# Row-by-row output projection of a cross-attention block, in a fixed order, in front of a SwiGLU layer

## The chip, the cores and the metric

The kernel runs on one core of one Trainium2 chip. The metric is the device time of one execution in microseconds (us). A core has five engines that run their own instruction streams: TensorE for matrix products and transpositions (PE in the profile, with PEld for its weight loads), VectorE (DVE), ScalarE (ACT), GpSimd (POOL) and SyncE (SP), which here only issues DMA transfers. Matrix products are written into PSUM, which the kernel uses as eight banks of 128 partitions x 512 numbers of 32 bits.

## The reference, cut to what matters

The reference is one encoder layer of width 1024 over 512 tokens: two mixers merged by gates, a cross-attention to 256 memory tokens, and a SwiGLU. The change touches the stretch from the softmax of the cross-attention to the first products of the SwiGLU:

```python
def memory_cross_attention(hn, memn, w_q, w_k, w_v, w_o):
    ...
    s = jnp.einsum('blhd,bmhd->bhlm', q, k).astype(jnp.float32) * (XATTN_HEAD_DIM ** -0.5)
    p = jax.nn.softmax(s, axis=-1).astype(v.dtype)
    o = jnp.einsum('bhlm,bmhd->blhd', p, v).reshape(bsz, seq, D_MODEL)
    return o @ w_o

def swiglu(hn, w_gate, w_up, w_down):
    return (jax.nn.silu(hn @ w_gate) * (hn @ w_up)) @ w_down
...
        h = h + memory_cross_attention(rms_norm(h, xattn_norm_g[i]), memn,
                                       w_q[i], w_k[i], w_v[i], w_xo[i])
        h = h + swiglu(rms_norm(h, ffn_norm_g[i]), w_gate[i], w_up[i], w_down[i])
```

Four heads of 256 are used; the SwiGLU is 2816 wide. `w_o` is called `w_xo` in the kernel.

## The kernel before, in words

**Number format.** Every operand of a product is split into a high part in a rounded 32-bit format and the rest. `split` (L80) does it: a cast on ScalarE (L85), then a subtraction on VectorE (L86) that needs the cast's result. `mm3` (L375) makes three matmuls of one product: high x high, high x low, low x high.

**Seven products in place of eight.** The large products are done in blocks of a 2 x 2 scheme with seven products instead of eight. In `w_xo`'s case each of the seven has a number q, which the comments and this text call P1 to P7. The sum of products that makes one quarter of the output is collected in PSUM, and `onto` (L1416) adds a pair of PSUM banks to two row blocks of the residual `h` (or subtracts them), on VectorE (L1421). Token rows come in four blocks of 128, t = 0 to 3; columns in two halves of 512. The sum in the banks `ox` that is subtracted from rows 2 and 3, second half, by `onto(ox, 2, 1, ALU.subtract)` is called U here.

**Order of the projection.** After heads 2 and 3 the products of `w_xo` run in this order, each in two parts c = 0 and 1 with a weight block of 256 x 512 each: P6 in `ox`, P5 in `oq`, P4 in `oy`, P2 in `ov`, P3 in `oq`. `oq` is begun by P5, added to rows 0 and 1, and then P3 is added on top of it in the same banks and the whole goes to rows 2 and 3. The PSUM pools have five banks for products (tag "mm": `ox`, `oq`, `ov`, later `pf`, `px`, `pv` and so on) and three auxiliary ones (tag "aux": `oy1` and the transpositions `ptr`). A new pair of banks has to wait until the tile that held the bank before has been read: `ov` takes the banks of `ox`.

**Norm and transposition.** As soon as a row block of `h` is complete, `half_done` squares and sums each half on ScalarE (`sum_sq`, L500). `to_fn(t, ...)` makes the norm factor on VectorE and GpSimd (L509 to L511), the scaled row `xs` on VectorE (two instructions, L526), and then, a little later by the kernel's own count of TensorE's time (`later`, `tick`), the transpositions: eight blocks of 128 x 128 in two auxiliary banks `ptr` (L534), each split into `fn` (L85, L86) and also copied whole to `full` by ScalarE (L538). A bank of `ptr` is free again when cast, subtraction and copy have read it.

**After it.** The SwiGLU begins with the rows 0 and 1 (`T0`): `gate_part(0, T0)` and `gate_part(1, T0)` (tile `pf`), and between them the first unit of the seven-product scheme (`px`, then `pv`). Then `between` (a matmul into a bank `idle`, L1567), the same gate blocks for rows 2 and 3, and a block of the up projection. The next products are `pq`.

**Who sets the order.** The kernel is written with a tile scheduler. The program text gives dependencies and priorities; a planner with costs of its own orders the instructions of each engine. Instructions passed through `in_order` keep, on their engine, the order of the program text among themselves. While `pinned[0]` is true, that holds for both halves of every `split`, for every square of `sum_sq`, and for the additions of `onto`; matmuls are pinned only where `mm3` is called with `turn`. `pinned[0]` becomes true before P6's last additions and false before the additions of P2's `ov` to rows 2 and 3.

**Weights.** `next_w` hands out the next weight block of one list, `plan`. It issues the loads that lie up to 15 blocks ahead, as far as each load's own lead allows (3 blocks for `w_xo`), and splits the blocks that lie up to 2 ahead. So a call of `next_w` also issues transfers on SyncE's queue and the two halves of a split on ScalarE and VectorE. Weight blocks of P4 to P7 are sums that were put in DRAM earlier (`xsum`); those of P2 and P3 come straight from `w_xo`. The tile names are `wraw` for the raw block, `whi` and `wlo` for its halves, `b11`, `b21`, `t`, `b22` for those of the SwiGLU units, and `s` for a block of w_gate that is kept split.

**Softmax.** `scores(hd)` multiplies each of the four rows of a head's exponentials by the reciprocal of their sum: on VectorE for heads 0 and 1 (L1274), on ScalarE for heads 2 and 3 (L1276).

Of the kernel before, what the change touches and what calls it, by code (L numbers as in the profile page):

```python
# [12 lines left out]
ALU = mybir.AluOpType  # L13
# [39 lines left out]
def hybrid_layer_kernel(  # L53
# [8 lines left out]
    nc = tc.nc  # L62
    x, mem, out = x[0], mem[0], out[0]
    w_in, w_glu, w_proj_a, w_proj_b, w_out = w_in[0], s5_w_glu[0], w_proj_a[0], w_proj_b[0], w_out[0]
    w_q, w_k, w_v, w_xo = w_q[0], w_k[0], w_v[0], w_xo[0]
# [11 lines left out]
    def bank(name):  # L77
        return pm.tile([P, 512], F32, tag="mm", name=name)
# [13 lines left out]
    pinned = [False]  # L92
    in_order = tc.keep_in_program_order
# [253 lines left out]
    def next_w(*key):  # L347
        i = used_w[0]
        used_w[0] += 1
        assert len(plan[i][0]) == len(key) and plan[i][0][1:] == key[1:] and plan[i][0][0] is key[0]  # L350
        for j in range(i, min(i + FAR + 1, len(plan))):
            begin(j, i)
            if j - 1 >= len(tiles) and j - 1 <= i + SPLITS:
                split_w(j - 1)
        for j in range(len(tiles), min(i + SPLITS + 1, len(plan))):
            split_w(j)
        tile_, tiles[i] = tiles[i], None
        return tile_

    def begin(j, i):  # L360

        loads = plan[j][1]
        while loads and j - loads[0][0] <= i:
            loads.pop(0)[1]()
# [4 lines left out]
    def split_w(j):  # L369
        tiles.append(plan[j][2]())  # L370

    def mm3(ps, a, b, start, stop, free=False, turn=False):

        for i, (x, y) in enumerate(((0, 0), (0, 1), (1, 0))):
            m = nc.tensor.matmul(ps, a[x], b[y], start=start and i == 0, stop=stop and i == 2, skip_group_check=free)  # L375
            if turn:
                in_order(m)
# [26 lines left out]
    def feat_block(ps, x, act, nk, kpt, tsl, fresh=True):  # L404

        kb, hi, lo = x
        for j in range(2):
            cs = slice(j * P, (j + 1) * P)
            for k in range(kpt):
                kk = kb + k  # L410
                mm3(ps[j][:, tsl], (hi[:, k, cs], lo[:, k, cs]), (act[0][:, kk, tsl], act[1][:, kk, tsl]),
                    kk == 0 and fresh, kk == nk - 1, not fresh)
# [57 lines left out]
    def tick(us=5.2):  # L470

        side["now"] += us / 5.2
        run_due()
        side["credit"] = min(side["credit"] + us * side["rate"], us)
        while side["credit"] > 0.0 and side["gen"] is not None:
            try:
                used = next(side["gen"])
            except StopIteration:
                side["gen"] = None
                return  # L480
            if used is None:
                side["credit"] = 0.0
                return
            side["credit"] -= used
# [13 lines left out]
    def sum_sq(dst, src):  # L498
        sq = np_.tile([P, 512], F32, tag="ev", name="sq", bufs=2)
        act = nc.scalar.activation(sq[:, :src.shape[-1]], src, AF.Square, accum_out=dst)  # L500
        if pinned[0]:
            in_order(act)
# [11 lines left out]
    HALF = (slice(0, 512), slice(512, 1024))  # L514
# [32 lines left out]
    def slot(tag, shape, dt, name):  # L547
        return sp.tile(list(shape), dt, tag=tag, name=name)
# [511 lines left out]
    for h in range(H):  # L1060
        ps = bank("psv")
# [84 lines left out]
    h = slot("A", (P, NT, D), F32, "h")  # L1146
# [27 lines left out]
    hss = cp.tile([P, 3, NT, 2], F32, name="hss")  # L1174
# [12 lines left out]
    def feat_norm(g, hi, lo, full=None, skip=False):  # L1187

        return lambda t, ss: norm_feat(h[:, t, :], g, hi, lo, slice(t * P, (t + 1) * P), ss, full,
                                       0 if skip and t >= 2 else None)  # L1190
# [60 lines left out]
    def scores(hd):  # L1251
        q_hi, q_lo = qs.pop(hd)
        scale = XD ** -0.5
        prob = ap_.tile([P, NT, M], F32, tag="prob", name="prob", bufs=1) if hd % 2 == 0 else \
            np_.tile([P, NT, M], F32, tag="gain", name="prob", bufs=2)
        for i in range(2):
            ps = bank("psc").rearrange("p (t m) -> p t m", t=2)
            for tt in range(2):
                t = 2 * i + tt
                tsl = slice(t * P, (t + 1) * P)  # L1260
                for k in range(2):
                    mm3(ps[:, tt, :], (q_hi[:, k, tsl], q_lo[:, k, tsl]),
                        (kt_hi[:, 2 * hd + k, :], kt_lo[:, 2 * hd + k, :]), k == 0, k == 1)
            mx, nm, sm, rs = (ap_.tile([P, 2], F32, tag=k, name=k, bufs=4) for k in ("mx", "nm", "sm", "rs"))
            nc.vector.tensor_reduce(mx, ps, AX.X, ALU.max)
            nc.vector.tensor_scalar(nm, mx, -scale, None, ALU.mult)
            for tt in range(2):
                nc.scalar.activation(prob[:, 2 * i + tt, :], ps[:, tt, :], AF.Exp, bias=nm[:, tt:tt + 1],
                                     scale=scale, accum_out=sm[:, tt:tt + 1])
            nc.vector.reciprocal(rs, sm)  # L1270
            for tt in range(2):
                row = prob[:, 2 * i + tt, :]
                if hd < 2:
                    nc.vector.tensor_scalar(row, row, rs[:, tt:tt + 1], None, ALU.mult)  # L1274
                else:
                    nc.scalar.activation(row, row, AF.Copy, scale=rs[:, tt:tt + 1])  # L1276
        return prob
# [20 lines left out]
    def product(ps, u, q, start, ops):  # L1298

        hi, lo = next_w(u[0], u[1], q)  # L1300
        for j in range(2):
            cs = slice(j * P, (j + 1) * P)
            for k in range(4):
                a = (hi[:, k, cs], lo[:, k, cs])
                b = (ops[q][0][:, k, :], ops[q][1][:, k, :])
                for i, (x, y) in enumerate(((0, 0), (0, 1), (1, 0))):
                    nc.tensor.matmul(ps[:, j, :], a[x], b[y], start=start and j == k == i == 0,  # L1307
                                     stop=k == 3 and i == 2, skip_group_check=True)
        tick(2.7)
# [95 lines left out]

    g_f = gain(ffn_norm_g[0], "g_f")

    def xo_product(ps, q, c, start, stop, w=None, ts=(0, 1)):
        hi, lo = w or next_w(w_xo, q, c)
        a = xops[q]  # L1410
        for t in ts:
            tsl = slice(t * P, (t + 1) * P)
            for k in range(2):
                mm3(ps[t], (a[0][:, 2 * c + k, tsl], a[1][:, 2 * c + k, tsl]), (hi[:, k, :], lo[:, k, :]),
                    start and k == 0, stop and k == 1, True)
        tick(1.35 * len(ts))  # L1416

    def onto(ps, t0, half, op):
        for t in range(2):
            hs = h[:, t0 + t, HALF[half]]  # L1420
            add = nc.vector.tensor_tensor(hs, hs, ps[t], op)  # L1421
            if pinned[0]:
                in_order(add)

    def half_done(t, half):
        sum_sq(hss[:, 1, t, half:half + 1], h[:, t, HALF[half]])
# [7 lines left out]
    ox = [bank("ox0"), bank("ox1")]  # L1434
# [19 lines left out]
    oq = [bank("oq0"), bank("oq1")]  # L1454
# [8 lines left out]
    for t in range(2):  # L1463
        half_done(t, 1)
    onto(ox, 0, 0, ALU.add)
    xo_product(oy, 4, 0, False, False)
    onto(ox, 2, 1, ALU.subtract)
    xo_product(oy, 4, 1, False, True)
    onto(oy, 0, 0, ALU.add)
    for t in range(2):  # L1470
# [5 lines left out]
    to_fn = feat_norm(g_f, fn_hi, fn_lo, full)  # L1476
    for t in range(2):
        to_fn(t, hss[:, 1, t, :])
    xo_product(ov, 2, 1, False, True)
    pinned[0] = False  # L1480
    onto(ov, 2, 0, ALU.add)
    for t in (2, 3):
        half_done(t, 0)
    ws = [next_w(w_xo, 3, c) for c in range(2)]
    for c in range(2):
        xo_product(oq, 3, c, False, c == 1, ws[c])
    onto(oq, 2, 1, ALU.add)
    for t in (2, 3):
        half_done(t, 1)
        to_fn(t, hss[:, 1, t, :])  # L1490

# [49 lines left out]
    def put(u, f, ts, src):  # L1543
        dst = acts(u[1] // 512, f)[:, :, ts]
        if u[0] is w_gate:
            nc.scalar.activation(dst, src, AF.Silu)
        else:
            nc.vector.tensor_tensor(dst, dst, src, ALU.mult)

    def unit_second(u, v):  # L1550
        product(v, u, 2, False, ops)
        put(u, 0, T0, v)
# [3 lines left out]
    ps = [bank("pf0"), bank("pf1")]  # L1556
    ws = []

    def gate_part(i, ts):
        if ts is T0:  # L1560
            ws.append((4 * i,) + next_w(w_gate, 4 * i, 4, FS, 256))
        feat_block(ps, ws[i], fn, KD, 4, ts, ts is T0)
        tick(2.7)

    def between():

        in_order(nc.tensor.matmul(aux("idle"), ops[1][0][:, 0, 0:P], fn_hi[:, 4, :], start=True, stop=True))  # L1567

    gate_part(0, T0)
    begun = unit_start(UNITS[0])  # L1570
    gate_part(1, T0)
    unit_second(UNITS[0], begun[1])
    between()
    for i in range(2):
# [53 lines left out]
    for i, u in enumerate(UNITS):  # L1628
        final = i == len(UNITS) - 1
        x, v = begun  # L1630
        q = unit_bank("pq")
# [164 lines left out]
```

## Time and profile before

| | us |
| --- | --- |
| median of 3 runs | 912.39 (910.86 to 913.31) |
| profiled execution | 911.88 |
| its span | 910.1 |
| PE busy | 890.3 (98%) |
| DVE busy | 641.6 (70%) |
| ACT busy | 491.0 (54%) |
| POOL busy | 111.9 (12%) |

The mean granted clock of TensorE over the span was 0.995 of full speed. Times inside the profile are microseconds from the start of the span. A row of the timeline has the start, the length, the engine, the line of the kernel, the operation, `output<-inputs`, the tile's shape, how many instructions the row holds, and in brackets the idle time before it and what ended that. A row of the waits has the waiting engine, tile and line, what it waited for, and then the total, the number and the longest. A row of the windows has the window, its length, then busy time and number of instructions for PE, PEld, DVE, ACT and POOL, TensorE's granted clock, the share of the DMA engines and GB/s.

The change lies between about 500 us (softmax of heads 2 and 3) and 612 us (first products of the SwiGLU). In the stretch from 540 to 612 the matmuls of `w_xo`, the transpositions and the first SwiGLU products follow each other on PE with five waits.

### The profile page before, as it was taken

The numbers are of one execution on the slowest core, as the hardware profiler recorded it, in microseconds if no ns is written. First come the engines' busy times: TensorE is split into PE (matmuls) and PEld (weight loads), VectorE is DVE, ScalarE is ACT, GpSimd is POOL, SyncE is SP. The second block draws the span as 40 slices with busy tenths as digits, with TensorE's granted clock in tenths as the row PEclk, the third lists the DMA queues.
The fourth block names the chain that finished last, engine by engine and source line by source line (L and its number), as shares of the span: only waits on it lengthen the run. The fifth ranks groups of instructions, "written<-read, shape, count | busy, mean of one in ns | idle before, by whom it ended". The sixth has DMA issues, their size and how long they took to land.

```text
span 910.1 us, 14545 instructions
## 1 busy us (share of the span) xinstructions
PE 890.3 (98%) x5619; PEld 784.7 (86%) x5619; DVE 641.6 (70%) x1040; ACT 491.0 (54%) x724; POOL 111.9 (12%) x173
## 2 busy tenths in 40 slices
PE   9999999999999999999999998899999999999996
PEld 6888888888888887889899987799999999986885
DVE  5696652888753235858956798866778777897875
ACT  5543985144364334347655785635455455654663
POOL 1004320110025200011001000101121011000010
PEclk9999999999999999999999999999999999999999
DMA  7567574586546578873568446718799998366673
GB/s 243 165 162 179 122 185 141 162 194 154 153 136 143 134 197 242 274 212 120 180 216 257 133 139 175 217 34 223 177 276 214 214 234 229 93 197 190 205 242 104
DMA packets 116167, 165.35 MB, mean 182 GB/s; under 512 B 13873, under 2 KB 78913, under 8 KB 116034
## 3 DMA queue, kind: packets, MB, share of 16 engines
q1 hardware_dynamic: 95234, 134.56, 46.0%
q0 software_dynamic: 18272, 28.81, 19.0%
q10 hardware_dynamic: 2592, 1.05, 0.4%
q8 instruction: 44, 0.72, 0.3%
q14 instruction: 25, 0.20, 0.1%
HBM read 157.61 MB, written 46.63 MB: 224 GB/s over the span
## 4 chain that ended last, share of the span: by engine, by line
PE 85%; ACT 5%; DVE 4%; DMA 3%; issue 2%; POOL 1%; ACTq 0%; POOLq 0%; SPq 0%; DVEq 0%
PE pf L375 27%; PE px L1307 12%; PE pt L375 11%; PE pq L1307 6%; PE dx L375 5%; PE pv L1307 3%; PE qx L1307 2%; PE dq L375 2%; PE pk L815 2%; DMA wraw<-dsum 1%; ACT whi L85 1%; DVE wlo L86 1%; PE ptr L534 1%; PE po L375 1%; PE ox L375 1%
## 5 line engine op out<-in xcount | busy, mean ns | idle before, releaser
L86 DVE TENSOR_TENSOR wlo<-wraw,whi 128x1024 fp32r<-128x1024 f32 (+1 forms) x147 | 174.7, 1188 | 106.1 <-ACT whi L85 104.3
L85 ACT CAST whi<-wraw 128x1024 fp32r<-128x1024 f32 (+1 forms) x147 | 150.4, 1025 | 166.7 <-PE pf L375 70.5
L375 PE MATMUL pf<-xn,whi 128*128 128x512 f32 x448 | 140.1, 392 | 0.0
L375 PEld LDWEIGHTS pf<-xn,whi 128*128 128x128 f32 x448 | 83.4, 188 | 17.1 <-issue 0.2
L375 PE MATMUL pf<-xn,wlo 128*128 128x512 f32 x224 | 87.4, 390 | 0.0
L1307 PE MATMUL px<-fn,whi 128*128 128x256 f32 x480 | 83.2, 276 | 0.0
L1307 PEld LDWEIGHTS px<-fn,whi 128*128 128x128 f32 x480 | 72.7, 188 | 0.2
L85 ACT CAST whi<-b 128x1024 fp32r<-128x1024 f32 x40 | 42.1, 1054 | 49.3 <-PE px L1307 27.8
L86 DVE TENSOR_TENSOR wlo<-b,whi 128x1024 fp32r<-128x1024 f32 x40 | 48.8, 1221 | 26.0 <-ACT whi L85 26.0
L1307 PE MATMUL px<-fn,wlo 128*128 128x256 f32 x240 | 66.3, 276 | 0.0
L1307 PE MATMUL pq<-s,whi 128*128 128x256 f32 x320 | 55.0, 276 | 0.0
L375 PE MATMUL dx<-whi,s 128*128 128x512 f32 x170 | 53.6, 391 | 0.4 <-ACT whi L85 0.4
L85 ACT CAST whi<-t 128x1024 fp32r<-128x1024 f32 x30 | 31.6, 1053 | 34.1 <-PE pv L1307 10.6
L86 DVE TENSOR_TENSOR wlo<-t,whi 128x1024 fp32r<-128x1024 f32 x30 | 36.7, 1224 | 18.7 <-ACT whi L85 18.7
L375 PEld LDWEIGHTS pf<-xn,wlo 128*128 128x128 f32 x224 | 42.1, 188 | 8.7
L1307 PEld LDWEIGHTS pq<-s,whi 128*128 128x128 f32 x320 | 48.3, 188 | 0.0
L1307 PEld LDWEIGHTS px<-fn,wlo 128*128 128x128 f32 x240 | 45.1, 188 | 0.0
L1307 PE MATMUL pq<-s,wlo 128*128 128x256 f32 x160 | 44.2, 276 | 0.0
L375 PE MATMUL pt<-whi,xn 128*128 128x512 f32 x128 | 43.6, 412 | 0.1
L375 PEld LDWEIGHTS dx<-whi,s 128*128 128x128 f32 x170 | 31.8, 188 | 7.4 <-ACT whi L85 0.8
L375 PE MATMUL dx<-wlo,s 128*128 128x512 f32 x85 | 32.9, 390 | 0.0
L295 POOL DMA_DIRECT2D dsum<-in_w_down_dram x12 | 13.9, 1158 | 134.9 <-DMA dsum<-in_w_down_dram 130.1
(456 smaller groups left out, 2266.4 us busy)
## 6 DMA issues: line engine op xcount, KB each, us to landing
wraw<-in_w_in_dram SPq DMA_DIRECT2D x36, 512.0 KB, 4.6
dsum<-in_w_down_dram SPq DMA_DIRECT2D x20, 512.0 KB, 5.3
wraw<-dsum SPq DMA_DIRECT2D x20, 512.0 KB, 4.1
b<-in_w_gate_dram SPq DMA_DIRECT2D x15, 512.0 KB, 4.7
b<-in_w_up_dram SPq DMA_DIRECT2D x15, 512.0 KB, 4.9
wraw<-in_w_down_dram SPq DMA_DIRECT2D x15, 512.0 KB, 4.8
dsum<-in_w_down_dram POOLq DMA_DIRECT2D x10, 512.0 KB, 7.6
dsum<-dsum POOLq DMA_DIRECT2D x10, 512.0 KB, 7.8
```

The costliest lines, as they stand in the source:

```text
L85: hi = nc.scalar.copy(dst_hi, src)
L86: lo = nc.vector.tensor_tensor(dst_lo, src, dst_hi.bitcast(F32), ALU.subtract)
L295: plan[j + step][1].append((0, lambda d=dst, x=more: nc.gpsimd.dma_start(d, x, accum_op=ALU.add)))
L375: m = nc.tensor.matmul(ps, a[x], b[y], start=start and i == 0, stop=stop and i == 2, skip_group_check=free)
L534: nc.tensor.transpose(ps[:, j, :], src[:, k * P:(k + 1) * P], ident)
L815: nc.tensor.matmul(ps[32 * j:32 * j + 32, q, :], bd[i][:, g].rearrange("p d c -> p (d c)"), lc(es[i], g), start=(i == 0), stop=False, tile ...
L1307: nc.tensor.matmul(ps[:, j, :], a[x], b[y], start=start and j == k == i == 0, stop=k == 3 and i == 2, skip_group_check=True)
```

## The change

Five things are done:

1. In `scores`, heads 2 and 3, the first row of each pair is scaled on VectorE and only the second on ScalarE: four of the eight scalings change the engine.
2. `xo_product` takes `turn` and passes it to `mm3`, so that its matmuls can be pinned.
3. U, `onto(ox, 2, 1, ALU.subtract)`, stands ahead of P4's first part instead of behind it. It is pinned in both versions.
4. P3 is done row by row. For row 2, then row 3: square the first half, do both parts of P3 for this row with pinned matmuls, add the row's bank of `oq` to `h` (pinned), square the second half, and call `to_fn` for the row. Both weight blocks of P3 are taken in the first of the two rounds, one ahead of each part. Before, both rows' first halves were squared, both weights taken, both parts done for both rows, both rows added, and then both rows normed.
5. `pinned[0]` becomes false only after `gate_part(1, T0)`. So from the additions of `ov` to rows 2 and 3 up to there, the additions, the squares of rows 2 and 3, and both halves of all splits are pinned in the order of the program text: those of the weights that `next_w` splits, and those of the transposed blocks of `fn`.

The numbers of products, transfers and element operations stay the same.

```diff
-                if hd < 2:
+                if hd < 2 or tt == 0:
                     nc.vector.tensor_scalar(row, row, rs[:, tt:tt + 1], None, ALU.mult)
                 else:
                     nc.scalar.activation(row, row, AF.Copy, scale=rs[:, tt:tt + 1])
...
-    def xo_product(ps, q, c, start, stop, w=None, ts=(0, 1)):
+    def xo_product(ps, q, c, start, stop, w=None, ts=(0, 1), turn=False):
...
-                    start and k == 0, stop and k == 1, True)
+                    start and k == 0, stop and k == 1, True, turn)
...
     onto(ox, 0, 0, ALU.add)
+    onto(ox, 2, 1, ALU.subtract)
     xo_product(oy, 4, 0, False, False)
-    onto(ox, 2, 1, ALU.subtract)
     xo_product(oy, 4, 1, False, True)
...
     xo_product(ov, 2, 1, False, True)
-    pinned[0] = False
     onto(ov, 2, 0, ALU.add)
-    for t in (2, 3):
-        half_done(t, 0)
-    ws = [next_w(w_xo, 3, c) for c in range(2)]
-    for c in range(2):
-        xo_product(oq, 3, c, False, c == 1, ws[c])
-    onto(oq, 2, 1, ALU.add)
-    for t in (2, 3):
-        half_done(t, 1)
-        to_fn(t, hss[:, 1, t, :])
+
+    ws = []
+    for t in range(2):
+        half_done(2 + t, 0)
+        for c in range(2):
+            if t == 0:
+                ws.append(next_w(w_xo, 3, c))
+            xo_product(oq, 3, c, False, c == 1, ws[c], (t,), True)
+        hs = h[:, 2 + t, HALF[1]]
+        in_order(nc.vector.tensor_tensor(hs, hs, oq[t], ALU.add))
+        half_done(2 + t, 1)
+        to_fn(2 + t, hss[:, 1, 2 + t, :])
...
     gate_part(0, T0)
     begun = unit_start(UNITS[0])
     gate_part(1, T0)
+    pinned[0] = False
     unit_second(UNITS[0], begun[1])
     between()
```

`xo_product` already had `ts`, the rows that it works on, and `mm3` already had `turn`.

## The prediction

> **What bounds the kernel now.** I read the page first, then the PE waits between 540 and 612 us (the only stretch in which the change alters the order of any engine), then the same stretch in windows, and then the rows of each engine in it. First the page: busy time by engine.
>
> ```profile
> span 910.1 us, 14545 instructions
> PE 890.3 (98%) x5619; PEld 784.7 (86%) x5619; DVE 641.6 (70%) x1040; ACT 491.0 (54%) x724; POOL 111.9 (12%) x173
> ```
>
> PE is busy for 98% of the span, so a change that leaves the number of matmuls alone can only win or lose where PE waits. The waits of PE from 540 to 612, with the total, the number and the longest:
>
> ```profile
> engine line waited for: us in total, times, longest us
> PE pf L375 <- ACT fn L85: 3.3, 1, 3.3
> PE ov L375 <- DVE h L1421: 1.8, 1, 1.8
> PE idle L1567 <- ACT fn L85: 0.7, 1, 0.7
> PE oq L375 <- DVE wlo L86: 0.5, 1, 0.5
> PE ptr L534 <- ACT full L538: 0.3, 1, 0.3
> ```
>
> They sum to 6.6 us. The same stretch in windows; PEclk is the granted clock:
>
> ```profile
> 556.70:564.00 7.30, 5.51 (x25) 4.56 (x25) 6.58 (x13) 3.96 (x8) 1.10 (x2) 1.00 0.48 152
> 584.90:591.30 6.40, 2.47 (x10) 1.75 (x8) 5.64 (x7) 5.46 (x9) 1.32 (x1) 0.68 1.04 243
> 591.30:596.00 4.70, 4.70 (x31) 4.70 (x30) 1.30 (x2) 1.28 (x2) 0.00 (x0) 0.71 0.11 17
> 608.70:640.00 31.30, 31.30 (x279) 31.30 (x278) 22.21 (x23) 17.08 (x21) 2.48 (x2) 1.00 0.73 188
> ```
>
> Two things are to be seen. From 608.7 on PE is busy without a gap, and the order there is unchanged, so whatever delay or lead PE has at 608.7 reaches the end of the kernel. And the clock falls to half for a while after the 3.3 us wait (0.68 and 0.71), but not after the 1.8 us wait (1.00 in the first row). PE's rows at the turning points, with start, length and idle before:
>
> ```profile
> 558.53 0.47 PE L375 MATMUL ov<-whi,ot_hi 128*128 128x512 f32 x1 [1.79 <-DVE h L1421]
> 564.09 0.62 PE L375 MATMUL oq<-whi,ot_hi 128*128 128x512 f32 x2
> 564.55 1.48 PE L534 MATMUL ptr<-ident,xs 128*128 128x128 f32 x12
> 578.18 2.88 PE L375 MATMUL pf<-fn,s 128*128 128x256 f32 x24
> 591.30 4.19 PE L375 MATMUL pf<-fn,s 128*128 128x256 f32 x24
> 608.70 0.39 PE L1307 MATMUL pq<-s,whi 128*128 128x256 f32 x2
> ```
>
> 24 matmuls of 256 columns take 2.88 us, and 4.19 us in the slow stretch. Below, one of 256 counts 0.1135 us and one of 512 counts 0.2275 (24 from 558.53 to 564.09, 5.56 us, first ones a little slower). DVE and ACT in the stretch:
>
> ```profile
> 553.53 1.28 DVE L1421 TENSOR_TENSOR h<-h,oq 128x512 f32<-128x512 f32 x2
> 556.56 1.23 DVE L86 TENSOR_TENSOR wlo<-wraw,whi 128x1024 fp32r<-128x1024 f32 x1 [0.55 <-ACT whi L85]
> 557.70 1.28 DVE L1421 TENSOR_TENSOR h<-h,ox 128x512 f32<-128x512 f32 x2
> 560.03 1.28 DVE L1421 TENSOR_TENSOR h<-h,oy 128x512 f32<-128x512 f32 x2
> 562.65 1.41 DVE L526 SCALAR_TENSOR_TENSOR xs<-h,r,g_f 128x512 f32<-128x512 f32 x2
> 563.98 0.68 DVE L1421 TENSOR_TENSOR h<-h,ov 128x512 f32<-128x512 f32 x1
> 569.91 1.87 DVE L86 TENSOR_TENSOR fn<-ptr,fn 128x512 fp32r<-128x512 f32 x3
> ...
> 544.86 0.34 SPq L242 DMA_DIRECT2D wraw<-xsum  x1
> ...
> 550.08 1.06 ACT L85 CAST whi<-wraw 128x1024 fp32r<-128x1024 f32 x1 [2.69 <-DMA wraw<-xsum]
> 560.80 0.63 ACT L500 ACTIVATE sq<-h 128x512 f32<-128x512 f32 x1 [3.33 <-DVE h L1421]
> 563.99 1.05 ACT L85 CAST s<-wraw 128x1024 fp32r<-128x1024 f32 x1
> 565.58 1.54 ACT L85 CAST fn<-ptr 128x512 fp32r<-128x512 f32 x3
> 571.92 1.06 ACT L538 COPY full<-ptr 128x512 f32<-128x512 f32 x2
> ```
>
> An addition onto h takes 0.68 alone and 0.60 in a row (1.28 for two), a DVE half of a weight split 1.23 (1.14 to the next), an ACT half 1.05 (0.95), a cast of a transposed block 0.5, its DVE half 0.6 to 0.68, the copy `full` 0.49 to 0.59, a square 0.63. From the squares' start to the first `xs` it is 1.85 us (560.80 to 562.65).
>
> **Part 1: scaling of the probabilities.** Four of ScalarE's eight scalings go to VectorE.
>
> ```profile
> L1274 DVE TENSOR_SCALAR prob<-prob,rs x8: 346/348/354, 498.7 to 516.9; 128x256 f32<-128x256 f32 x8
> L1276 ACT ACTIVATE prob<-prob,rs x8: 493/518/545, 519.3 to 526.7; 128x256 f32<-128x256 f32 x8
> ```
>
> That is 4 x 0.52 = 2.1 us off ACT and 4 x 0.35 = 1.4 us onto DVE, between 519 and 527. PE's only waits in 540 to 612 are the five above, so any lead gained before 540 is worth only what part 2's waits leave of it; I count 0, at most 0.2 either way.
>
> **Part 2: U ahead of P4, the ov banks.** PE waits 1.79 us at 558.53 because `ov` takes the banks of `ox`, and those come free when U, the two additions at 557.70, has read them. In the new order U follows at once on the four additions at 553.53 and after. The queue ahead: the (4,1) weight lands for the cast at 550.08, its DVE half ends at about 552.4, and six additions run 552.3 to 556.0. So the banks are free at 555.4 and 556.0, before PE is through with P4 (556.6). But the DVE half of the first `ov` weight now stands behind U: it starts at 555.9 and ends at 557.15, where `ov` needs it at its third matmul. The wait of 1.79 becomes about 0.9 at 557.15. Then 22 matmuls x 0.2275 = 5.0: `oq` starts at 562.15 instead of 564.09. **Gain 1.9.**
>
> **Part 3: row by row, all pinned.** This is what decides. The additions of P4 run at 558.2, the first `xs` follows 2.62 later as before (560.03 to 562.65), 560.8, two more behind it, then the two weight halves for P3 with the fourth `xs` between them (to 565.7), and only then the additions of `ov` (565.7 to 566.9), which stood among the `xs` at 563.98 before. PE starts `oq` at 562.15, does 12 transpositions (3 blocks) and 5 `oq` matmuls to 565.2, with 0.4 lost at the weight half at 564.0 (0.5 before). Then in the fixed order stands the fourth block's transposition. It needs one of three aux banks, and the first block's bank is held until its cast, the cast's DVE half and the copy `full` are through. These are now held on ACT behind the square of row 2, which waits for the `ov` addition (566.4). From there, each step behind the one before: square 566.4 to 567.1, cast of the `s` weight (it is next in the fixed order) to 568.0, block cast to 568.6; on DVE the `s` half 568.1 to 569.3, the block's half to 570.0; on ACT `full` 570.0 to 570.6. Before, the casts of three blocks ran at 565.58 and nothing pinned held them. So PE stands from 565.2 to 570.6: **a new wait of 5.4 us**, with all of P3's other matmuls behind it.
>
> The next three blocks go cast, half, copy in turn, 0.50 + 0.68 + 0.59 + handing over = 1.82 us each; the last `full` starts at 575.45, the first up/gate weight's cast follows (to 577.0), its DVE half to 578.2, and only then the addition of P3's row 2 (578.2). PE meanwhile: 18 `oq` to 575.1, 24 `pf` to 577.8, first unit to 580.8. Row 2: square 578.9, +1.85: `xs` 580.7; the pinned addition of row 3 at 582.0; square 582.75, +1.85: `xs` 584.6 and 585.3; the second `s` half 585.9 to 587.1; then two blocks' rounds of 1.82, cast and half of the next weight (590.1 to 592.4). PE needs that half for the third matmul of `pv`: 592.4. Its waits between 580.8 and 592.4 come in pieces that sum to some 6.7 us (592.4 - 570.6 = 21.8, less 18 x 0.2275, 76 x 0.1135 and 20 transpositions x 0.12 from the twelve in 1.48), the longest 1.95 and 1.44. The 3.3 and 0.7 us waits of before are gone.
>
> From 592.4 PE has 164 matmuls of 256 and one of 512 columns (the two units' second halves and the gate and up parts, counted in the program) before the first `pq`: 164 x 0.1135 + 0.23 = 18.85, so 611.2 against 608.70: **+2.5**.
>
> **Clock.** 0.68 over 6.40 us and 0.71 over 4.70 us mean half clock from about 587.2 to 594.0, beginning some 2 us into the long wait:
>
> ```profile
> 588.38 0.80 PE L375 MATMUL pf<-fn,s 128*128 128x256 f32 x2 [3.26 <-ACT fn L85]
> ```
>
> It cost at most half of the 2.47 us that PE was busy before 591.3, 1.2, and 0.29 x 4.70 = 1.4 behind it: 2.6 in all. In the new order the clock should drop in the 5.4 us wait too, but the slow matmuls behind it run into the waits up to 592.4 and cost nothing. From 581 to 592.4 PE is busy 4 to 5 of 11 us, the same two fifths as from 584.9 to 591.3, where the clock fell. How far a slow stretch reaches past 592.4 sets its price: 0 if it has ended or was never entered, 1.4 as in the row of 591.3, 2.6 if it is entered at the last waits. The nearest row is 1.4; the waits come in smaller pieces than the 3.3 there, so I take 0.9.
>
> The Trainium skill's page "TensorE: Matmul & The Clock Gate" (section "Part 1: The HAM clock gate") has one idle window of some 3.4 us drop the clock and about as long of steady work restore it. By that rule pieces of at most 1.95 us drop nothing here, the tail is 0 and the sum 914.4 (rival 2); the trace agrees in that 1.79 dropped nothing, and leans against it in that the clock fell about 2 us into the wait.
>
> **Smaller parts.** Pinning xo_product's matmuls moves none in time where DVE and ACT bind; 0. SP: the `wraw` load of (4,1) was issued at 544.86, now behind another load of w_xo that goes ahead of the gate weights; the cast took it at 550.08. Taken as unmoved; each us later adds 1 us to all that follows from 552.4, and it could be at most 1.15 earlier, since its issue still waits for the DVE half of a weight used before. Range -1.15 to +2.
>
> **The sum.** Up to the start of `oq`: -1.9. From there to the first `pq` it was 608.70 - 564.09 = 44.6 us, of which 0.48 + 0.35 + 3.26 + 0.67 = 4.8 were waits, 2.6 the half clock, 37.2 work. Now it is 611.2 - 562.15 = 49.0: 0.4 + 5.4 + 6.7 = 12.5 of waits and 36.5 of work at full rate (0.7 less than in the trace, whose matmuls behind a wait are slower; most of that falls into the waits). So -1.9 + 7.7 - 2.6 - 0.7 = +2.5, and +0.9 for the clock: 911.9 + 3.4 = **915.3**, against the profiled execution of before (911.88 us, span 910.1). The median of the runs shown, 912.39, lies 0.5 above that execution.
>
> **Rivals.**
> 1. *The bank comes free in time; faster.* If ACT and DVE take row 2's additions and square early enough that the first `full` ends by 565.2, the 5.4 and what follows from it is gone; ov's 1.9 is kept (910.0), and with all of 0.5 + 0.3 + 3.3 + 0.7 and the 2.6 of the half clock, 902.6 at best. It decides at `full` ending 565.2; against it stands that the square waits for the last `ov` matmul (562 at the earliest) and for four `xs` and two weight halves ahead of it on DVE (4.9 us). Likeliest value if so 909. Chance 0.10.
> 2. *No late slow clock.* The first slow stretch is absorbed and no second one reaches past 592.4: 911.9 + 2.5 = 914.4. For it: the longest piece, 1.95, is close to the 1.79 that dropped nothing. Chance 0.27.
> 3. *A full late slow stretch or a late load.* +2.6 for the clock, or +1 to +2 for (4,1): 916.4 to 917.5. For it: PE is idle 60% of the time up to 592.4, and SP's order was changed. Chance 0.20.
> 4. *It does nothing that counts.* ACT and DVE hide both the lost and the gained waits: 911.5 to 912.5. Against it: the bank wait lies on PE itself. Chance 0.05.
>
> **How the numbers follow.** My forecast, 914.6 to 916.2 around 915.3, has 0.38. A measurement of this kernel tells about 0.3%, 2.7 us, from no change. Faster: rival 1, 0.10. Same: rival 4 and most of rival 2, with the low end of the forecast (up to 915.1 by the median): 0.05 + 0.20 + 0.07 = 0.32. Slower: the rest, 0.58. Range: leaving out most of rival 1 and the top of rival 3 gives 911.2 to 918.0.
>
> **What would show it.** Right: the wait of `ov` at L1421 gone or under 1 us and `oq` starting near 562; a PE wait of about 5 us at `ptr` L534 on ACT `full` L538 near 565 to 571; the 3.3 us wait of `pf` gone; many waits of 0.3 to 2 us between 580 and 593; the first `pq` near 611 to 612. Wrong: `full` of the first block ending before 566; `ptr` waiting under 2 us; the cast of (4,1) elsewhere than 550; a clock of 1.00 throughout 565 to 600, or of half behind 594.

## The result and the profile after

The changed kernel takes 914.76 us (median of 13 runs, 912.53 to 916.18) against 911.36 us of the kernel before (13 runs): a ratio of 1.0030, 95% interval 1.0019 to 1.0040. It is slower by 3.4 us. 915.3 was forecast, with "slower" as the likeliest side.

The waits of TensorE from 540 to 615 us in the changed kernel (waiting engine and tile, what it waited for, then total, number, longest):

```profile
PE ptr L534 <- ACT full L538: 5.2, 1, 5.2
PE pf L375 <- DVE s L86: 1.1, 1, 1.1
PE pf L375 <- ACT s L85: 1.0, 1, 1.0
PE oq L375 <- DVE wlo L86: 0.5, 1, 0.5
PE ptr L534 <- DVE xs L526: 0.3, 1, 0.3
PE pv L1307 <- DVE wlo L86: 0.2, 1, 0.2
```

The wait of `ov` (1.8 us) is gone and so is that of `pf` on the cast of `fn` (3.3 us). In their place stands one wait of 5.2 us: the fourth transposed block has no bank until the first block's copy to `full` is through. The waits sum to 8.3 us, against 6.6 before.

TensorE's rows at the turning points of the changed kernel:

```profile
556.72 0.62 PE L375 MATMUL ov<-whi,ot_hi 128*128 128x512 f32 x2
562.19 0.50 PE L375 MATMUL oq<-whi,ot_hi 128*128 128x512 f32 x1
571.59 1.11 PE L534 MATMUL ptr<-ident,xs 128*128 128x128 f32 x4 [5.21 <-ACT full L538]
588.31 4.15 PE L375 MATMUL pf<-fn,s 128*128 128x256 f32 x20 [1.08 <-DVE s L86]
593.56 0.38 PE L1307 MATMUL pv<-fn,wlo 128*128 128x256 f32 x1 [0.17 <-DVE wlo L86]
612.62 0.39 PE L1307 MATMUL pq<-s,whi 128*128 128x256 f32 x2
```

`oq` starts at 562.19 instead of 564.09, but the first `pq` at 612.62 instead of 608.70. So 1.9 us were won up to `oq` and 5.8 lost behind it. The chain that set this, on ScalarE and then on VectorE:

```profile
556.86 1.05 ACT L85 CAST whi<-wraw 128x1024 fp32r<-128x1024 f32 x1 [1.93 <-DMA wraw<-in_w_xo_dram]
567.40 0.63 ACT L500 ACTIVATE sq<-h 128x512 f32<-128x512 f32 x1 [4.33 <-DVE h L1421]
568.03 1.03 ACT L85 CAST s<-wraw 128x1024 fp32r<-128x1024 f32 x1
568.97 0.58 ACT L85 CAST fn<-ptr 128x512 fp32r<-128x512 f32 x1
570.95 0.59 ACT L538 COPY full<-ptr 128x512 f32<-128x512 f32 x1 [1.41 <-DVE fn L86]
576.93 1.05 ACT L85 CAST whi<-b 128x1024 fp32r<-128x1024 f32 x1
...
553.13 2.47 DVE L1421 TENSOR_TENSOR h<-h,ox 128x512 f32<-128x512 f32 x4
559.08 1.28 DVE L1421 TENSOR_TENSOR h<-h,oy 128x512 f32<-128x512 f32 x2
566.63 1.28 DVE L1421 TENSOR_TENSOR h<-h,ov 128x512 f32<-128x512 f32 x2
579.16 0.68 DVE L1490 TENSOR_TENSOR h<-h,oq 128x512 f32<-128x512 f32 x1
592.28 1.23 DVE L86 TENSOR_TENSOR wlo<-b,whi 128x1024 fp32r<-128x1024 f32 x1 [1.59 <-ACT whi L85]
```

Read them in order of time. The four additions at 553.13 end with U, so the banks are free for `ov`. The first three transposed blocks are written into `ptr` from 562.60 to 564.5, but ScalarE stands idle for 4.33 us in front of row 2's square, because that square comes first in the fixed order and needs the `ov` additions of 566.63. The cast of the first block starts at 568.97 (565.58 before), its copy at 570.95. Then a round of cast, half and copy takes 1.83 us per block, until the cast of the next weight starts at 576.93 and row 2's addition of P3 at 579.16. The half of a weight at 592.28 is the last thing that TensorE waits for.

The granted clock (fourth number; window, length, busy time with the count, then clock, DMA share and GB/s), in windows of 1.5 us of the changed kernel:

```profile
573.00:574.50 1.50, 1.50 (x5) 0.50 0.35 122
588.00:589.50 1.50, 1.19 (x8) 0.81 0.07 6
589.50:591.00 1.50, 1.50 (x9) 0.50 0.75 238
```

Half clock stood twice: from about 568.4 to 575.3, in and behind the 5.2 us wait, and from about 588.9 to 592.3. Both ended before the last wait at 593.56.

In the profiles of all these kernels the last `psc` matmul starts between 516.6 and 520.2 us, although up to 515 the order on TensorE, VectorE, ScalarE and GpSimd is the same in all of them, and the down projection behind 800 also differs by up to 3 us. So for the experiments two numbers are given: the median, and the stretch from the start of the last `psc` matmul (scores, ahead of everything that the change moves) to the start of the first `pq`. For before and after, the rows with the first and the last start of each group:

```profile
L375 PE MATMUL psc<-kt_hi,qq x64: 276/276/369, 481.5 to 518.1; 128*128 128x256 f32 x64
L1307 PE MATMUL pq<-s,whi x320: 276/276/281, 608.7 to 799.3; 128*128 128x256 f32 x160
...
L375 PE MATMUL psc<-kt_hi,qq x64: 276/276/369, 482.0 to 518.7; 128*128 128x256 f32 x64
L1307 PE MATMUL pq<-s,whi x320: 276/276/281, 612.6 to 803.3; 128*128 128x256 f32 x160
```

That is 608.7 - 518.1 = 90.6 us before and 612.6 - 518.7 = 93.9 after: +3.3.

In both profiled executions of U alone (913.62 and 914.20 us) the stage of the units, 580 to 800, ran some 3.5% slower at a shown clock of 1.00 (197.5 us from the first to the last start of `pq`, 190.6 before), so their rows behind 580 are not used.

One more thing has to be set beside the 5.2 us wait. This is the fourth block before:

```profile
572.55 0.66 PE L534 MATMUL ptr<-ident,xs 128*128 128x128 f32 x4 [0.35 <-ACT full L538]
```

Before, too, it starts as soon as the first block's copy has ended, and that is 54.4 us behind the last `psc` (572.55 - 518.14). In the changed kernel it is 52.9 us (571.59 - 518.68). So the bank does not come free later than before, but 1.5 us earlier. What is new is the work that TensorE has done by then: six of P3's 24 matmuls, where before all 24 stood ahead of the block. From the fourth block to the first `pq` it is then 41.0 us, against 36.2 before; 18 matmuls of P3 that come in here, some 4.1 us, and the chain above are in that.

### The profile page after: what moved, and what is told of

It is laid out like the page before. It is cut to its first block, busy times and chain, and to the rows that moved or that the text cites. A ratio compares the mean times of both kernels' runs of the same rounds, so it can differ in the third digit from the quotient of the medians.

```text
span 913.0 us, 14542 instructions
## 1 busy us (share of the span) xinstructions
PE 891.5 (98%) x5619; PEld 787.0 (86%) x5619; DVE 643.4 (70%) x1044; ACT 489.9 (54%) x720; POOL 111.9 (12%) x173
## 4 chain that ended last, share of the span: by engine, by line
PE 84%; DVE 5%; ACT 5%; DMA 2%; issue 2%; POOL 1%; POOLq 0%; SPq 0%; ACTq 0%; DVEq 0%
PE pf L375 27%; PE px L1307 12%; PE pt L375 11%; PE pq L1307 6%; PE dx L375 5%; PE dq L375 3%; PE pv L1307 3%; PE qx L1307 2%; DVE wlo L86 2%; PE pk L815 2%; PE dv L375 1%; ACT whi L85 1%; PE psc L375 1%; PE qq L1307 1%; DMA wraw<-dsum 1%
## 5 line engine op out<-in xcount | busy, mean ns | idle before, releaser
L1307 PE MATMUL pq<-s,wlo 128*128 128x256 f32 x160 | 44.2, 276 | 0.0
L1307 PEld LDWEIGHTS pq<-s,wlo 128*128 128x128 f32 x160 | 30.1, 188 | 0.0
```

## Experiments

Two theories of the loss. **P**: the late end of the pins is the cause. It fixes ScalarE's and VectorE's order so that casts of transposed blocks, which are ready, stand behind a square that is not. **T**: the row-by-row P3 with pinned matmuls is the cause; it puts a transposition between `oq` matmuls on TensorE. The transpositions themselves are not pinned in any version; the planner places them.

| kernel | us, median | ratio, 95% | `psc` to `pq`, us |
| --- | --- | --- | --- |
| changed | 914.76 | 1.0019 to 1.0040 | 93.9 |
| no_turn | 914.43 | 1.0003 to 1.0051 | 93.9 |
| late_pin | 911.87 | 0.9954 to 1.0016 | 90.5 |
| u_late_pin | 910.57 | 0.9924 to 0.9987 | 89.9 |
| early_unpin | 908.47 | 0.9904 to 0.9966 | 87.5 |
| fn_free | 908.15 | 0.9918 to 0.9975 | 87.7 |
| rows_no_u | 906.69 | 0.9889 to 0.9953 | 88.0 |
| scale_half | 908.14, again 910.50 | 0.9918 to 0.9997, 0.9946 to 1.0017 | 89.5, 89.3 |
| u_first | 904.40, again 905.25 | 0.9902 to 0.9966, 0.9880 to 0.9951 | not used |
| u_and_scale | 903.38, again 904.45 | 0.9813 to 0.9932, 0.9872 to 0.9937 | 84.4, 84.0 |

### early_unpin: the changed kernel with the pins ended early

```diff
     xo_product(ov, 2, 1, False, True)
+    pinned[0] = False
     onto(ov, 2, 0, ALU.add)
...
     gate_part(1, T0)
-    pinned[0] = False
```

> The changed kernel with the pins ended where the kernel before ended them (ahead of the additions of ov to rows 2 and 3); rows of P3 and their matmuls and additions stay as changed. Theory P (the late end of the pins on ScalarE's and VectorE's splits and squares makes the new wait of ptr): that wait of 5.2 us falls under 1 us and the time is 2 to 6 us under before (a wait of px on a weight of up to 4 us may come in its place). Theory T (the rows with pinned matmuls on TensorE make it): the wait stays at 4 to 5.5 us and the time stays 2.5 to 4 us over before.

```profile
PE px L1307 <- ACT whi L85: 3.2, 1, 3.2
...
571.52 0.58 ACT L538 COPY full<-ptr 128x512 f32<-128x512 f32 x1
572.15 0.92 PE L534 MATMUL ptr<-ident,xs 128*128 128x128 f32 x4
```

908.47 us, 6.3 under the changed kernel, with rows and pinned matmuls as there: for the time, P holds. A wait of `px` came in place of that on `full`: its weight's cast starts at 570.57, after 3.06 us in which ScalarE waited for the load.

For the wait, P holds only in name. The fourth block again has six of P3's 24 matmuls ahead of it, and it starts as the first block's copy ends, 52.3 us behind the last `psc` (52.9 in the changed kernel); the wait of `px` covers the same idle time. Of the 6.4 us that the stretch is shorter, 0.6 lie ahead of the fourth block and 5.8 behind it (35.2 us to the first `pq`, 41.0 in the changed kernel), where no wait of TensorE is listed any more.

### no_turn: the changed kernel without the pinned matmuls

```diff
-            xo_product(oq, 3, c, False, c == 1, ws[c], (t,), True)
+            xo_product(oq, 3, c, False, c == 1, ws[c], (t,))
```

> The changed kernel with the matmuls of P3 not pinned, all else as changed. Theory P: the planner may put more matmuls ahead of the fourth block, so the wait of ptr is shorter (1 to 3 us), but the chain on ScalarE and VectorE behind it is the same and the first pq starts within 1 us of where the changed kernel has it (612.6); time 2.5 to 4.5 us over before. Theory T: the chain is gone with the pins on TensorE, time at or under before.

```profile
PE pf L375 <- ACT fn L85: 1.8, 1, 1.8
PE pf L375 <- ACT s L85: 1.6, 1, 1.6
PE ptr L534 <- ACT full L538: 1.3, 1, 1.3
PE pf L375 <- DVE s L86: 1.1, 1, 1.1
```

914.43 us and 93.9 us in the stretch, just as the changed kernel. The planner now puts all 24 of P3's matmuls ahead of the block, so the 5.2 us falls to 1.3, but the rest comes back as other waits. So the pinned matmuls make the 5.2 us wait, and it costs nothing by itself: the chain on ScalarE and VectorE, which runs as in the changed kernel, sets the end. T falls as the cause of this loss.

### fn_free: the changed kernel, only the transposed blocks' splits left out of the pins

`split` takes one more argument; weights, squares and additions stay pinned.

```diff
-        if pinned[0]:
+        if pinned[0] and not free:
...
-                split(hi[:, 4 * q:4 * q + 4, tsl], lo[:, 4 * q:4 * q + 4, tsl], ps)
+                split(hi[:, 4 * q:4 * q + 4, tsl], lo[:, 4 * q:4 * q + 4, tsl], ps, True)
```

> The changed kernel, pins as late as there, but the two halves of the splits of the transposed blocks (fn) are left out of them; weights' splits, squares and additions stay pinned. If the wait of ptr comes from these casts being held behind row 2's square and the next weight's cast: the wait is under 1 us (one of pf on the first weight of up to 3 us may take its place), the first pq lies some 5 to 7 us earlier than in the changed kernel against the last psc, and the time is 906 to 909. If the other pins (weights, squares) hold ScalarE as well: the wait stays above 3 us and the time above 912.

```profile
PE pf L375 <- ACT s L85: 2.7, 1, 2.7
...
571.11 1.05 PE L534 MATMUL ptr<-ident,xs 128*128 128x128 f32 x4
```

908.15 us; the stretch is 6.2 us shorter than in the changed kernel. So of all that was pinned late, it is the casts and halves of the transposed blocks that cost, though squares and weights are still pinned. With them free, ScalarE casts the first three blocks together (from 564.66) and later copies them together (from 570.37), in place of one round of 1.83 us after the other. The fourth block starts 51.3 us behind the last `psc`, 1.6 earlier than in the changed kernel, and row 2's addition of P3 at 576.25, 56.5 us behind it, where the changed kernel has 60.5: 4.0 us earlier.

### late_pin and u_late_pin: the late pins with P3 as before

late_pin is the kernel before with only `pinned[0] = False` moved behind `gate_part(1, T0)`; u_late_pin has U ahead of P4 as well.

```diff
     xo_product(ov, 2, 1, False, True)
-    pinned[0] = False
...
     gate_part(1, T0)
+    pinned[0] = False
```

> The kernel before with only the end of the pins moved behind the second gate part; U, P3 and the scaling as before. Theory P: a new wait of ptr on ACT full of 2.5 to 5 us and several pieces of 0.4 to 2 us behind it, time 1 to 4 us over before. Theory T: no such wait, time within 1 us of before.

```profile
PE ptr L534 <- ACT full L538: 3.1, 1, 3.1
PE ov L375 <- DVE h L1421: 1.8, 1, 1.8
PE pf L375 <- ACT fn L85: 1.3, 1, 1.3
```

Half a miss. The wait on `full` came as P says (3.1 us), the loss did not: 911.87 against 912.57 us, no difference. The old waits of `pf` (3.3) and of `idle` (0.7) went at the same time, so one pair of waits stood in for another. That raised the question whether the pins cost only together with the rows:

> The kernel before with U ahead of P4 and the late end of the pins; P3 and the scaling as before. Theory P (the late pins cost by themselves what U gains): the wait of ptr on ACT full comes back at 3 to 4 us with pieces of 0.5 to 2 us behind it, and the time is 909 to 912, 5 to 8 us over U alone (904.4). Theory R (the pins cost only together with the row-by-row P3, since alone they left the kernel before unchanged at 911.9): time 903 to 907.

```profile
PE ptr L534 <- ACT full L538: 3.1, 1, 3.1
PE pf L375 <- ACT fn L85: 1.8, 1, 1.8
```

910.57 us, 5 to 6 us over U alone: the pins cost by themselves, as soon as the old wait that they replace is gone otherwise. The changed kernel, which adds the row-by-row order with its pinned matmuls and the scaling, is another 4 us slower (910.57 to 914.76; 89.9 to 93.9 in the stretch).

### u_first: U alone

```diff
+    onto(ox, 2, 1, ALU.subtract)
     xo_product(oy, 4, 0, False, False)
-    onto(ox, 2, 1, ALU.subtract)
```

> The kernel before with U alone moved ahead of P4's first part. Both theories: the wait of ov on the additions of L1421 (1.8 us) falls under 1 us and oq starts about 1 to 2 us earlier. If that lead is all, the time is some 1.5 to 2 us under before. By the order in which the planner now puts the instructions, row 2's part of the chain also moves: the wait of pf on ACT fn (3.3 us) and the half clock behind it should shrink to under 1 us, which would give 4 to 7 us under before. If the move is worthless (the wait only changes place), the time is within 0.5 us of before.

> U alone once more, for rows of an undisturbed execution: 903 to 906; ov waits under 1 us, pf on ACT fn under 0.5 us, clock 1.00 from 584 to 600.

904.40 and 905.25 us, 7 to 8 us under before, where 4 to 7 was the most that was expected: the largest gain of any part, and four times the 1.9 us that the bank wait holds. `ov` waits 0.6 us. `pf` on the cast of `fn` waits 0.2 us in the first profile and is not among the waits of the second, in place of 3.3; for the rest see the next kernel.

### u_and_scale, and scale_half

The kernel before with U ahead and half the scaling moved, and with the scaling alone.

```diff
-                if hd < 2:
+                if hd < 2 or tt == 0:
```

> The kernel before with U ahead of P4 and the scaling of half the rows on VectorE; P3 and the pins as before. If the scaling counts nothing: 903.5 to 905.5, as U alone (904.4). If it brings TensorE to P4 earlier by some tenths and nothing takes them back: 902.5 to 904. The wait of pf on ACT fn stays under 0.5 us.

> U and the scaling once more, as the fastest so far, with more rounds: 902 to 905, at or up to 1.5 us under U alone. If the scaling does nothing beside U, the two lie within 0.5 us of each other.

903.38 (4 runs) and 904.45 us (10 runs): beside U the scaling is worth less than these runs tell apart. It is the fastest version, with U alone next to it: some 8 us under before, 10 under the changed kernel. Its longest wait from 530 to 616 (second profile; two more have 0.5 and 0.4 us):

```profile
PE ptr L534 <- DVE xs L526: 0.5, 1, 0.5
```

Where the 3.3 us went is seen on ScalarE, first before, then u_and_scale (first profile):

```profile
584.41 1.05 ACT L85 CAST whi<-t 128x1024 fp32r<-128x1024 f32 x1
585.36 0.59 ACT L85 CAST fn<-ptr 128x512 fp32r<-128x512 f32 x1
585.96 1.28 ACT L1546 ACT_TABLE_LOAD   x1
587.75 0.58 ACT L85 CAST fn<-ptr 128x512 fp32r<-128x512 f32 x1
...
583.53 1.26 ACT L85 CAST fn<-ptr 128x512 fp32r<-128x512 f32 x2 [1.97 <-PE ptr L534]
585.36 0.59 ACT L85 CAST fn<-ptr 128x512 fp32r<-128x512 f32 x1
586.31 1.07 ACT L85 CAST whi<-t 128x1024 fp32r<-128x1024 f32 x1
587.40 1.28 ACT L1546 ACT_TABLE_LOAD   x1
```

Before, a weight's cast and a load of the activation table stood among the casts of rows 2 and 3's blocks, and TensorE waited for the one behind it. With U ahead, the planner put three of those casts in front of weight cast and table load. The two additions that were moved touch none of these instructions; the planner's order of all that follows changed. That this order makes the difference is read off the rows; no run set this order by itself.

> The kernel before with only the scaling of half the rows on VectorE. The wait of ov on the additions of L1421 stays (about 1.8 us, any lead goes into it), and that of pf on ACT fn too (3.3 us): time within 1 us of before. If the scaling carried part of the change's effect, it would move by more than 1.5 us.

> The scaling alone once more, since its first runs moved by more than was expected. If what the trace shows between the last psc and the first pq (1.1 us less than before) is all, the time is 910 to 911.5. If the first median (908.1) holds, 907 to 909: then 2 to 3 us of it lie in stretches whose order the edit does not touch.

908.14 and then 910.50 us; 1.1 and 1.3 us less in the stretch. So about 1 us is the scaling's by the stretch; that the rest of the first median is its work too is not shown, and the second median does not have it. Its longest wait, second profile, is the old one:

```profile
PE pf L375 <- ACT fn L85: 3.3, 1, 3.3
```

`ov` on L1421, 1.8 us before, waits 0.3 in the first profile and is not among the waits of the second. That was expected to stay, and was a miss: in the new order P6's last matmul starts 30.6 us after the last `psc` instead of 33.2, the additions follow, and the banks come free earlier without U being moved: `ov` starts 38.5 and 38.3 us after the last `psc`, 40.4 before.

### rows_no_u: early pins, rows, no U

early_unpin with the two lines of U put back in their old order.

> The changed kernel with the pins ended early and U put back behind P4's first part; rows of P3 and scaling as changed. If U still counts in that order: the wait of ov (1.5 to 2 us) is back and the time is 1 to 2 us over early_unpin's 908.5, 909.5 to 910.5. If the wait of px on its weight (3.2 us, set by the load) swallows it: px waits 1.5 to 2 us less and the time is 908 to 909.

906.69 us, 88.0 us in the stretch against early_unpin's 87.5. Neither branch fits: `ov` waits only 0.4 us (the scaling has taken that wait already) and `px` still 3.1. The medians stand the other way round than the stretches and their intervals overlap; U is worth at most half a us in this order. Row by row with early pins and U, which is early_unpin, is 4 us behind u_and_scale by the medians and 3.1 to 3.5 by the stretch. Its longest wait, 3.2 us, is that of `px`: one matmul of `px` stands ahead of 18 of P3's, at a moment when its weight has not been loaded. Whether the rows cost this, or the pinning of their matmuls, is open: no run has the rows with early pins and free matmuls.

## Why the prediction was right, point by point

**The total** was right (+3.4 forecast, +3.4 measured), but its closeness is luck: two terms were off and cancel, a late load that was not counted (+0.9) and the clock, counted 0.9 and worth 0.2.

**Part 2, the banks of `ov`, -1.9:** right in size (`oq` started at 562.19, 562.15 forecast), but by luck as to the cause. The scaling alone, counted 0 in part 1, brings `ov` 1.9 to 2.1 us earlier against the last `psc` and takes most of its wait; U then adds little: rows_no_u, which lacks U, starts `oq` 44.2 us behind the last `psc`, early_unpin 43.5, before 46.0. The prediction also left some 0.9 us of wait at the third matmul of `ov`. By its own times it would have been 0.1 (P4 ends at 556.6, two matmuls later it is 557.06, the weight half ends at 557.15), and there was none.

**Part 3, the new wait, 5.4:** right in size, place and chain: 5.2 us, at the block, by the `full` copy and in the order that was named. That free casts had the bank free earlier before, as its comparison suggests, is not borne out: against the last `psc` they ran 2.9 us earlier then, yet the bank came free 1.5 us later. The wait is there because six of P3's matmuls stand ahead of the block instead of 24. The prediction calls that place part of the fixed order; it is the planner's, and follows the pinned matmuls (no_turn has 24). What the late pins cost is the chain behind the block, as early_unpin and fn_free show, and the sum had this right, since it goes by the end of that chain. The wait lay 1 us later (566.4 to 571.6 instead of 565.2 to 570.6). The step that was off is the loads: (4,1) was taken as unmoved, and its cast ran at 549.71 (550.08 before), but the *next* load, of P2's second weight, held ScalarE for 1.93 us until 556.86. The additions of `oy` began at 559.08 instead of 558.2, +0.9 on all that followed.

**The rest of the chain** ran as worked out: rounds of 1.83 us (1.82), last half of a weight ending at 593.5 (592.4 and the 0.9). Its pieces of wait were forecast at 6.7 us and came to 2.6 (1.1 + 1.0 + 0.3 + 0.2), mostly because slow matmuls filled the others: 3.6 us at half clock behind 571.6 and 3.4 from 588.9 are 3.5 us of work lost, by estimate, that would have been waited for anyway.

**The clock, +0.9:** wrong in size. From the last wait to the first `pq` it was 612.62 - 593.56 = 19.06 us, against 18.85 at full rate: 0.2. The first slow stretch was absorbed, as said. The second did come, as the share of busy time suggested, but it ended at 592.3, before the last wait. So rival 2's "none reaches past" described the outcome better than the forecast did; its 914.4 and the 0.9 of the load make 915.3, as near to the measured time as the forecast. The Trainium skill's page "TensorE: Matmul & The Clock Gate" (section "Part 1: The HAM clock gate") has one idle window of some 3.4 us drop the clock. The second stretch does not bear that out: the waits ahead of it were 1.00, 0.28 and 1.08 us.

**"Whatever PE has at 608.7 reaches the end":** nearly. The 3.9 us at the first `pq` still stood at the first `dq` (808.2 to 812.1), and the span is 2.9 longer: in the profiled pair the down projection gave 1.0 back.

**Part 1, counted 0:** wrong alone (1.1 to 1.3 us), and here its reason did not hold: the scaling itself shortens the wait of `ov`, as said under part 2. What its own part in the changed kernel's total is, no run shows.

**What the sum hid.** The prediction priced U by the wait that it removes. Alone, U brings 7 to 8 us; the planner's order then also lacks the 3.3 us wait and its slow stretch. The 3.4 us are thus a balance: the changed kernel gives up some 10 us that two of its five parts would have won, about 6 by the late pins and 4 by the rows with their pinned matmuls.

## What to carry to other kernels

Before pinning a list of instructions on an engine, look for the first in it that waits for a late result: everything behind it, ready or not, inherits that wait, and work that could be done in one go is done in rounds. A long wait in the list is not yet the cause of a loss: here the 5.2 us shrank to 1.3 in no_turn and the time stayed, because another chain set the end. Where a planner orders the rest, price an edit by the order that it makes afterwards, and test each part of a bundle alone: here the best version is two of the five parts.

## What the hardware showed that was not expected

The clock fell to half at about 588.9 after three short waits (1.00, 0.28, 1.08 us, with 2.5 of 4.5 us busy from 583.5 to 588.0), while one wait of 1.79 us before had not lowered it, and in late_pin a wait of 3.10 us lowered it only about as it ended (1.00 from 571 to 574, 0.52 from 574 to 577). Each slow stretch lasted 3.4 or 6.8 us, and the changes of the clock in the changed kernel, at about 568.4, 575.3, 588.9 and 592.3, lie some 6.9, 13.6 and 3.4 us apart, about two, four and one times 3.4. In the 3.4 us ahead of the two falls TensorE was busy for 1.35 us and for 1.98 us, 0.6 of the latter with transpositions, so it was not idle throughout; from 556.5 to 559.9 before, around the 1.79 us wait, it was busy for 1.62 us and the clock did not fall. What share decides, and whether transpositions count less, no run here shows. In the changed kernel, where ScalarE and VectorE set the end, TensorE took only 0.2 us more than at full rate from the last wait to the first `pq`, so the two stretches before it cost little.
